# The expert-product stage of a two-block transformer kernel: gelu half a unit later, all low parts on VectorE, picks and token pairs spread over other blocks

## The chip, the cores and the metric

The kernel runs on one core of one Trainium2 chip. The metric is the device time of one execution in microseconds (us). Three runs of the kernel before gave 2947.26, 2949.1 and 2950.67 us.

## What is computed

The reference is a small model of two blocks for 256 tokens of width 2048. Nearly all of it is untouched here; the change lies in the last part, a feed-forward layer that takes for each token 16 of 16384 experts in each of 8 heads:

```python
q = (hf @ w_pq).reshape(T, PEER_HEADS, 2, PEER_HALF)
s1, s2 = ...                                     # scores against two sets of 128 keys
v1, i1 = lax.top_k(s1, 16); v2, i2 = lax.top_k(s2, 16)
cand = (v1[..., :, None] + v2[..., None, :]).reshape(T, PEER_HEADS, 256)
sc, ci = lax.top_k(cand, 16)                     # the picks
experts = e1 * 128 + e2                          # 128 experts per token
gates = softmax(sc)
...
u = jnp.take(w_u, experts); a = einsum('td,tkd->tk', h, u)
c = gates * gelu(a)
y = einsum('tk,tkd->td', c, jnp.take(w_v, experts))
```

## The kernel before

The kernel does not gather rows of `w_u`. It forms the product of all 16384 experts with all 256 tokens (this is the "u stage"), keeps gelu of it in a large table `C` of 128 partitions (first key of the expert) by 128 columns `e2` (second key) by 256 tokens, and multiplies the table by a sparse table of gates. After that, rows of `C` that are not empty are sent to memory in a compacted order, and their rows of `w_v` are gathered and multiplied.

**Units and blocks of the u stage.** The loop `u_block(e2)` runs over 128 units. A unit has two blocks `b` = 0 and 1, so there are 256 blocks; block `i` is `2 * e2 + b`. A block is a weight tile of 128 x 1024. It is loaded from `w_u` by SP into a buffer `wr`, ScalarE copies it to a rounded high part `wh` (L1464), and another engine subtracts to get the low part `wl` (L1469). There are four `wr`, two `wh` and two `wl` buffers. TensorE (PE) then runs eight matmuls of 512 columns with the high part and eight of 256 columns with the low part into a PSUM tile `P`. The high part of block `i + 1` is ordered by `split_next(i + 1)` at the start of block `i`, its low part by `low()` inside `between` of block `i`.

**End of a unit.** After its second block, ScalarE copies half of `P` to `a` (L1502, "the evacuation"), VectorE adds the other half (L1503), and GpSimd multiplies by the row scale (L1504; from the time when all gates are placed VectorE does it). `a` has two buffers, `rbc` and `junk`. The gelu of `a` is written by `tail()` (L1481 for tokens that have no gates yet, L1483 for the others, followed by a multiply into `C` at L1484 on GpSimd, later VectorE).

**`between`.** Once per block the kernel puts a portion of other work beside the matmuls:

- *Picks*: the top-16 searches on VectorE (L1350 to L1420), with the candidate sums on GpSimd (L1388). The generator gives a weight with each step: 45 for one head of 128 tokens (16 such) and 86 for the decoding of four heads (4 such), 1064 in all. A block takes steps until 18 units are used. Six further blocks hold the last of the gates' preparation (`finish`).
- *Pairs*: when the picks are done, each block makes one pair of tokens: `pair_ops` builds one-hot rows (six VectorE operations L1516 to L1518 and four ScalarE copies L1521 per pair), and the next block starts with `pair_mms`, eight small matmuls. Every second pair completes four tokens, and `quad_end` multiplies them into the rows of `C` that have their gelu (L1537 on VectorE) and copies the others (L1539 on ScalarE). 128 pairs take 128 blocks.
- *Places and sends*: when all 64 groups of four are done, `places` works out where the rows go, and GpSimd sends the rows of `C` (`send`, L1584), six per unit in the program, each waiting for nothing but its own row.

**The order of work** on PE, ScalarE and VectorE is the program order (`manual_schedule`): an instruction that waits holds up all behind it on its engine. GpSimd and SP have in-order queues of their own.

In the kernel before the low part of the second block of a unit is made by GpSimd while picks are under way, in seven units of eight; all others are made by VectorE.

Of the kernel before, what the change touches and what calls it, by code (L numbers as in the profile page):

```python
# [10 lines left out]
F32 = mybir.dt.float32  # L11
# [5 lines left out]
OP = mybir.AluOpType  # L17
# [1265 lines left out]
def peer(nc, tc, io, xd, hT, rbc, hp, sp, W, ident, mm, raw_block, split_block, proj_T, blocks, power_rstd, new_pair):  # L1283
    cd = io["cd"]
    with ExitStack() as es:
# [35 lines left out]
        with ExitStack() as pu_stack:  # L1321
# [132 lines left out]
            parts, tails, done = {}, [], [0]  # L1454
            q4 = 0

            def split_next(i):

                e2, b = divmod(i, 2)
                if e2 == 128:  # L1460
                    return lambda: None
                raw = raw_block(io["w_u"][e2, b])
                hi = W["pool"].tile([128, 1024], F32R, name="wh", bufs=W["hi"])
                nc.scalar.activation(hi, raw, AF.Copy)  # L1464
                eng = nc.gpsimd if b and not topk_done and e2 % 8 else nc.vector

                def low():
                    lo = W["pool"].tile([128, 1024], F32R, name="wl", bufs=W["lo"])
                    eng.tensor_tensor(lo, raw, hi.bitcast(F32), op=OP.subtract)  # L1469
                    parts[i] = hi, lo  # L1470

                return low

            def tail():

                if tails:
                    e2, a = tails.pop()
                    done[0] = e2 + 1
                    nt = 4 * q4
                    if nt < 256:  # L1480
                        nc.scalar.activation(C[:, e2, nt:256], a[:, nt:], AF.Gelu_apprx_tanh)  # L1481
                    if nt:
                        nc.scalar.activation(a[:, :nt], a[:, :nt], AF.Gelu_apprx_tanh)  # L1483
                        (nc.gpsimd if nt < 256 else nc.vector).tensor_tensor(  # L1484
                            C[:, e2, :nt], C[:, e2, :nt], a[:, :nt], op=OP.mult)

            def u_block(e2):
                P = pu.tile([128, 512], F32, name="pp")
                for b in range(2):
                    low = split_next(2 * e2 + b + 1)  # L1490
                    if b == 0:
                        tail()
                    between(low)
                    hi, lo = parts.pop(2 * e2 + b)
                    for j in range(8):
                        k = 8 * b + j
                        mm(P, hi[:, j * 128:(j + 1) * 128], hT[k].rearrange("p s t -> p (s t)"), k == 0, False)
                    for j in range(8):
                        k = 8 * b + j
                        mm(P[:, :256], lo[:, j * 128:(j + 1) * 128], hT[k][:, 0, :], False, k == KT - 1)  # L1500
                a = ua[e2 % 2]
                nc.scalar.activation(a, P[:, 256:], AF.Copy)  # L1502
                nc.vector.tensor_tensor(a, a, P[:, :256], op=OP.add)  # L1503
                (nc.gpsimd if q4 < 64 else nc.vector).tensor_tensor(a, a, rbc, op=OP.mult)  # L1504
                tails.append((e2, a))
# [3 lines left out]
            bank4 = [None]  # L1509
# [15 lines left out]
            def pair_mms(p, ws):  # L1525
                if p % 2 == 0:
                    bank4[0] = pq.tile([128, 4, 128], F32, name="pq")
                for i, w in enumerate(ws):
                    t = 2 * p + i
                    for a in range(3):  # L1530
                        mm(bank4[0][:, t % 4, :], w[:, 0, :], w[:, 1 + a, :], t % 4 == 0 and a == 0, t % 4 == 3 and a == 2)
                    mm(cnt[:, t // 128, :], w[:, 0, :], w[:, 4, :], t == 0, t == 255)

            def quad_end(q4, n):
                t4 = slice(4 * q4, 4 * q4 + 4)
                v = bank4[0].rearrange("p t e -> p e t")
                nc.vector.tensor_tensor(C[:, :n, t4], C[:, :n, t4], v[:, :n], op=OP.mult)  # L1537
                if n < 128:
                    nc.scalar.activation(C[:, n:, t4], v[:, n:], AF.Copy)  # L1539
# [50 lines left out]
            topk_done = False  # L1590
            left = 0
            pair, waiting = 0, []
            placing = None

            def between(low):


                nonlocal pair, q4, left, topk_done, placing
                if not topk_done or fins:
                    low()  # L1600
                    if fins and next(fins[0], "end") == "end":
                        fins.pop(0)
                        if topk_done:

                            nc.vector.tensor_scalar(C[:, :, 256:257].bitcast(I32).rearrange("p a o -> p (a o)"), iob,
                                                    128.0, row, op0=OP.mult, op1=OP.add)
                    left += 18
                    while left > 0 and not topk_done:
                        w = next(steps, None)
                        topk_done = w is None  # L1610
                        left -= w or 0
                    return
                full = None
                if waiting:
                    p, ws = waiting.pop()
                    pair_mms(p, ws)
                    if p % 2:
                        full = p // 2
                if pair < 128:
                    waiting.append((pair, pair_ops(pair)))  # L1620
                    pair += 1
                low()
                if placing and next(placing, "end") == "end":
                    placing = False
                if full is not None:
                    quad_end(full, done[0])
                    q4 += 1
                    if q4 == 64:
                        placing = places()
                        next(placing)  # L1630
# [68 lines left out]
        for i, e2 in enumerate(range(NC, 128)):  # L1699
            c2 = c_place()  # L1700
            halves(c2, C[:, e2, :256])
            for b in range(2):
                hi, lo = split_block(io["w_v"][e2 * 128:(e2 + 1) * 128, b * 1024:(b + 1) * 1024])
# [19 lines left out]
        def packed(j, tbs):  # L1723
            c2, v, off = fetch(j, tbs)
            for b in range(2):
                hi, lo = split_half(v, b)
                product(c2, b, hi, lo, tbs, off=off)
            return v

        def halves_of(j):  # L1730
            return tuple(tb for tb, (a, z) in enumerate((FIRST, SECOND)) if a <= j < z)
# [12 lines left out]
        for i, j in enumerate(order):  # L1744
            v = packed(j, halves_of(j))
# [7 lines left out]
        for i, j in enumerate(last_js):  # L1753
            c2, v, _ = fetch(j, (0, 1), vp.tile([128, 2, 256], F32R, name="lc", bufs=2))
# [9 lines left out]
        for tb in range(2):  # L1764
            t = slice(tb * 128, (tb + 1) * 128)
            y = xg[tb].rearrange("p (c n) -> p c n", c=4)
            ss = sp.tile([128, 2, 4], F32, name="xss", bufs=5)[:, 0, :]
            for c in range(4):
                for i, (c2, ws) in enumerate(last):
                    hi, lo = ws[c // 2]  # L1770
                    w = slice(c % 2 * 512, (c % 2 + 1) * 512)
# [119 lines left out]
```

## Time and profile before

| | us |
|---|---|
| median of three runs | 2949.1 |
| the profiled execution | 2950.48 |
| its span (first to last instruction) | 2948.7 |

| engine | busy in the span |
|---|---|
| PE (matmul) | 2768.1 us, 94% |
| VectorE (DVE) | 1898.4 us, 64% |
| ScalarE (ACT) | 1588.6 us, 54% |
| GpSimd (POOL) | 798.5 us, 27% |

The u stage lies between about 1537 and 2486 us of the span. A window of a stage gives for each engine the busy time in that stage; a wait is told as "who <- what it waited for"; in a timeline the number in brackets is the time that the engine sat idle just before, and what ended that. The clock PEclk is the share of the full clock that was granted to PE.

### The profile page before, as it was taken

The numbers are of one execution on the slowest core, as the hardware profiler recorded it, in microseconds if no ns is written. First come the engines' busy times: TensorE is split into PE (matmuls) and PEld (weight loads), VectorE is DVE, ScalarE is ACT, GpSimd is POOL, SyncE is SP. The second block draws the span as 40 slices with busy tenths as digits, with TensorE's granted clock in tenths as the row PEclk, the third lists the DMA queues.
The fourth block names the chain that finished last, engine by engine and source line by source line (L and its number), as shares of the span: only waits on it lengthen the run. The fifth ranks groups of instructions, "written<-read, shape, count | busy, mean of one in ns | idle before, by whom it ended". The sixth has DMA issues, their size and how long they took to land. (4 is left out here: it accounts for less than half of the span.)

```text
span 2948.7 us, 41341 instructions
## 1 busy us (share of the span) xinstructions
PE 2768.1 (94%) x14566; PEld 2301.3 (78%) x14566; DVE 1898.4 (64%) x3498; ACT 1588.6 (54%) x2951; POOL 798.5 (27%) x703
## 2 busy tenths in 40 slices
PE   8999999999999999999999899999994199999998
PEld 5867788887888888878887678888883087888886
DVE  7545576556766555565657878888882065766665
ACT  4445565445665544444544348888871054655554
POOL 6312320012310000111014442333337622322231
PEclk9999999999999999999999999999997599999999
DMA  6565443654446655666554344444445266988883
GB/s 224 177 223 189 134 139 123 218 187 154 147 144 208 209 183 167 215 211 193 183 179 157 134 157 158 159 158 161 160 144 189 98 216 236 359 298 285 299 308 133
DMA packets 158810, 561.74 MB, mean 191 GB/s; under 512 B 19584, under 2 KB 33536, under 8 KB 145024
## 3 DMA queue, kind: packets, MB, share of 16 engines
q1 hardware_dynamic: 137808, 433.71, 44.9%
q0 software_dynamic: 20784, 125.29, 11.4%
q8 instruction: 117, 1.92, 0.3%
q14 instruction: 101, 0.83, 0.1%
HBM read 531.17 MB, written 27.75 MB: 190 GB/s over the span
## 5 line engine op out<-in xcount | busy, mean ns | idle before, releaser
L204 DVE TENSOR_TENSOR wl<-wr,wh 128x1024 fp32r<-128x1024 f32 (+1 forms) x467 | 600.2, 1287 | 458.9 <-ACT wh L202 385.3
L187 PE MATMUL pp<-hT,wh 128*128 128x512 f32 x2880 | 754.4, 404 | 104.2 <-ACT wh L1464 53.3
L202 ACT ACTIVATE wh<-wr 128x1024 fp32r<-128x1024 f32 (+1 forms) x467 | 492.9, 1056 | 585.0 <-PE pp L187 495.5
L187 PE MATMUL pp<-wh,hT 128*128 128x512 f32 x2688 | 695.6, 399 | 4.6 <-ACT wh L202 2.7
L187 PEld LDWEIGHTS pp<-hT,wh 128*128 128x128 f32 x2880 | 525.0, 192 | 207.3 <-ACT wh L1464 58.8
L187 PEld LDWEIGHTS pp<-wh,hT 128*128 128x128 f32 x2688 | 501.3, 190 | 127.7 <-ACT wh L202 7.8
L187 PEld LDWEIGHTS pp<-hT,wl 128*128 128x128 f32 x2880 | 396.6, 192 | 57.8 <-issue 21.1
L187 PE MATMUL pp<-hT,wl 128*128 128x256 f32 x2880 | 406.6, 284 | 26.2 <-issue 20.3
L187 PE MATMUL pp<-wl,hT 128*128 128x512 f32 x1344 | 374.5, 400 | 12.1 <-DVE wl L204 12.1
L1469 DVE TENSOR_TENSOR wl<-wr,wh 128x1024 fp32r<-128x1024 f32 x230 | 278.7, 1221 | 116.3 <-issue 64.3
L187 PEld LDWEIGHTS pp<-wl,hT 128*128 128x128 f32 x1344 | 248.9, 190 | 70.6 <-DVE wl L204 15.4
L1464 ACT ACTIVATE wh<-wr 128x1024 fp32r<-128x1024 f32 x256 | 268.9, 1050 | 42.1 <-remote 33.1
L1676 ACT ACTIVATE hT<-vb 128x1024 fp32r<-128x1024 f32 x202 | 210.7, 1059 | 131.0 <-PE py L187 100.6
L1683 DVE TENSOR_TENSOR wr<-vb,hT 128x1024 fp32r<-128x1024 f32 x135 | 165.3, 1229 | 76.1 <-PE py L187 55.0
L1714 POOL DMA_INDIRECT vb<-w_v,cb x103 | 128.9, 1252 | 284.1 <-ACT hT L1676 99.7
L1584 POOL DMA_INDIRECT cd<-C,posi x124 | 137.6, 1110 | 138.0 <-DVE C L1484 89.5
L1521 ACT ACTIVATE oh<-oh,gP 128x128 bf16<-128x128 bf16 x512 | 162.0, 389 | 0.0
L187 PE MATMUL py<-hT,c 128*128 128x512 f32 x600 | 152.6, 389 | 0.0
L187 PE MATMUL py<-hT 128*128 128x512 f32 x592 | 150.4, 389 | 0.0
L187 PEld LDWEIGHTS py<-hT,c 128*128 128x128 f32 x600 | 112.6, 188 | 23.4
L187 PEld LDWEIGHTS py<-hT 128*128 128x128 f32 x592 | 111.1, 188 | 23.1
L1683 DVE TENSOR_TENSOR wl<-vb,hT 128x1024 fp32r<-128x1024 f32 x67 | 82.2, 1227 | 34.2 <-PE py L187 27.7
(445 smaller groups left out, 3162.4 us busy)
## 6 DMA issues: line engine op xcount, KB each, us to landing
wr<-w_u SPq DMA_DIRECT2D x256, 512.0 KB
wr<-w_even SPq DMA_DIRECT2D x104, 512.0 KB
wr<-w_out SPq DMA_DIRECT2D x96, 512.0 KB
wr<-w_odd SPq DMA_DIRECT2D x96, 512.0 KB
wr<-w_in SPq DMA_DIRECT2D x64, 512.0 KB
wr<-w_mem SPq DMA_DIRECT2D x32, 512.0 KB
wr<-w_pq SPq DMA_DIRECT2D x32, 512.0 KB
cb<-cd SPq DMA_DIRECT2D x103, 136.0 KB
```

What stands on the lines that cost most here:

```text
L187: nc.tensor.matmul(out, lhsT=lhsT, rhs=rhs, start=start, stop=stop, skip_group_check=True)
L202: nc.scalar.activation(hi, raw, AF.Copy)
L204: (lo_eng or nc.vector).tensor_tensor(lo, raw, hi.bitcast(F32), op=OP.subtract)
L1464: nc.scalar.activation(hi, raw, AF.Copy)
L1469: eng.tensor_tensor(lo, raw, hi.bitcast(F32), op=OP.subtract)
L1521: nc.scalar.activation(w[:, 1 + a, :], w[:, 4, :], AF.Copy, scale=gP[:, a, t:t + 1])
L1584: i = nc.gpsimd.indirect_dma_start(cd, bass.IndirectOffsetOnAxis(posi[:, e2:e2 + 1], 0), src, None).ins
L1676: nc.scalar.activation(hi, src, AF.Copy)
L1683: nc.vector.tensor_tensor(lo, src, hi.bitcast(F32), op=OP.subtract)
L1714: nc.gpsimd.indirect_dma_start(v, None, wide, bass.IndirectOffsetOnAxis(c[:, 256:257].bitcast(I32), 0))
```

## The change

The change has four parts, all in the u stage.

1. `tail()`, which writes the gelu of the unit before, is called in the second block of a unit instead of the first, again just behind the high part of the next block.
2. All low parts are made by VectorE.
3. The picks use 14 units per block instead of 18. By the weights they take 76 blocks (38 units) instead of 60, and the preparation of the gates ends at block 82 instead of 65.
4. Pairs start at block 83 instead of 66 and are spread so that 128 of them are made by block 193, the second block of unit 96. That is 111 blocks, of which 17 make two pairs. A block may start with two `pair_mms`. `pair_mms` returns its PSUM bank, since the next four tokens may already have begun another one when `quad_end` runs.

The last pair's matmuls stand at the start of block 194 in both kernels, and so do `places` and the first sends of the program.

```diff
@@ split_next
-                eng = nc.gpsimd if b and not topk_done and e2 % 8 else nc.vector
                 def low():
-                    eng.tensor_tensor(lo, raw, hi.bitcast(F32), op=OP.subtract)
+                    nc.vector.tensor_tensor(lo, raw, hi.bitcast(F32), op=OP.subtract)
@@ u_block
                     low = split_next(2 * e2 + b + 1)
-                    if b == 0:
+                    if b:
                         tail()
-                    between(low)
+                    between(2 * e2 + b, low)
@@ pair_mms, quad_end
+                return bank4[0]
-            def quad_end(q4, n):
+            def quad_end(q4, bank, n):
-                v = bank4[0].rearrange("p t e -> p e t")
+                v = bank.rearrange("p t e -> p e t")
@@ between
+            q_end = 2 * 97
-                    left += 18
+                    left += 14
...
-                full = None
-                if waiting:
-                    p, ws = waiting.pop()
-                    pair_mms(p, ws)
+                full, ws = [], list(waiting)
+                waiting.clear()
+                if pair < 128 and q_from is None:
+                    q_from = i
+                for p, w in ws:
+                    b4 = pair_mms(p, w)
                     if p % 2:
-                        full = p // 2
-                if pair < 128:
+                        full.append((p // 2, b4))
+                while pair < 128 and pair * (q_end - q_from) < 128 * (i + 1 - q_from):
                     waiting.append((pair, pair_ops(pair)))
                     pair += 1
                 low()
...
-                if full is not None:
-                    quad_end(full, done[0])
+                for p, b4 in full:
+                    quad_end(p, b4, done[0])
                     q4 += 1
```

## Rows read from the trace of the kernel before

**Rows 1.** Windows: picks, pairs, sends, rest; per engine busy us (instructions), clock, DMA.

```profile
1536.80:1769.00 232.20, 205.19 (x1112) 175.50 (x1111) 183.01 (x551) 96.62 (x147) 104.82 (x91) 0.96 0.45 150
1769.00:2195.00 426.00, 425.85 (x3075) 376.76 (x3073) 375.18 (x1026) 353.03 (x894) 144.18 (x126) 1.00 0.47 158
2195.00:2363.30 168.30, 63.79 (x311) 53.29 (x309) 36.49 (x59) 25.19 (x38) 105.81 (x106) 0.66 0.42 144
2363.30:2486.00 122.70, 122.70 (x705) 107.95 (x704) 78.98 (x113) 63.30 (x92) 33.54 (x20) 1.00 0.63 211
```

**Rows 2.** Timeline of PE: first high-part matmuls of blocks 0, 66 and 194.

```profile
1536.83 2.00 PE L187 MATMUL pp<-hT,wh 128*128 128x512 f32 x8
...
1769.03 1.32 PE L187 MATMUL pp<-hT,wh 128*128 128x512 f32 x5
...
2195.00 2.08 PE L187 MATMUL pp<-hT,wh 128*128 128x512 f32 x8
```

**Rows 3.** Waits while picks run (1536.8 to 1769 us): total us, times, longest.

```profile
ACT C L1481 <- POOL rbc L1504: 64.2, 16, 6.7
...
PE pp L187 <- ACT wh L1464: 26.5, 23, 3.4
...
DVE C L1350 <- POOL C L1388: 14.4, 10, 2.9
```

**Rows 4.** Timeline, all engines: from the end of unit 10 to block 24.

```profile
1613.88 0.40 DVE L1503 TENSOR_TENSOR rbc<-rbc,pp 128x256 f32<-128x256 f32 x1
...
1614.36 0.73 POOL L1504 TENSOR_TENSOR rbc<-rbc 128x256 f32<-128x256 f32 x1 [1.96 <-DVE rbc L1503]
...
1615.12 0.42 ACT L1481 ACTIVATE C<-rbc 128x256 f32<-128x256 f32 x1 [5.48 <-POOL rbc L1504]
...
1616.54 3.27 PE L187 MATMUL pp<-hT,wh 128*128 128x512 f32 x8 [2.20 <-ACT wh L1464]
```

**Rows 5.** Lines while picks run: busy us, mean ns of one, idle time before.

```profile
L1469 DVE TENSOR_TENSOR wl<-wr,wh 128x1024 fp32r<-128x1024 f32 x40 | 49.1, 1226 | 30.6 <-ACT wh L1464 30.6
L1417 DVE TENSOR_TENSOR C<-C 128x1024 bf16<-128x1024 bf16 x8 | 13.8, 1726 | 0.1
...
L1469 POOL TENSOR_TENSOR wl<-wr,wh 128x1024 fp32r<-128x1024 f32 x26 | 66.2, 2548 | 72.6 <-ACT wh L1464 72.6
```

**Rows 6.** Line L1417 by itself: shortest, median and longest ns.

```profile
L1417 DVE TENSOR_TENSOR C<-C x8: 684/1612/2895, 1576.9 to 1745.7; 128x1024 bf16<-128x1024 bf16 x8
```

**Rows 7.** Timeline, all engines, in one unit of the pair stage.

```profile
2175.30 0.42 DVE L1503 TENSOR_TENSOR junk<-junk,pp 128x256 f32<-128x256 f32 x1 [0.47 <-ACT junk L1502]
...
2175.80 0.79 DVE L1517 TENSOR_SCALAR oh<-iob,eT 128x128 bf16<-128x128 bf16 x1
...
2177.22 1.84 POOL L1484 TENSOR_TENSOR C<-C,junk 128x240 f32<-128x240 f32 x1 [0.68 <-ACT junk L1483]
...
2178.42 0.53 DVE L1537 TENSOR_TENSOR C<-C,pq 128x376 f32<-128x376 f32 x1
2178.87 0.24 DVE L1516 TENSOR_SCALAR oh<-iob,eT 128x128 bf16<-128x128 bf16 x1
2178.99 0.31 ACT L1539 ACTIVATE C<-pq 128x136 f32<-128x136 f32 x1 [0.73 <-DVE C L1537]
...
2180.12 1.26 ACT L1521 ACTIVATE oh<-oh,gP 128x128 bf16<-128x128 bf16 x4
2180.25 1.23 DVE L1469 TENSOR_TENSOR wl<-wr,wh 128x1024 fp32r<-128x1024 f32 x1 [0.19 <-ACT wh L1464]
...
2181.46 0.39 ACT L1502 ACTIVATE rbc<-pp 128x256 f32<-128x256 f32 x1
```

**Rows 8.** Timeline of the sends: the first, PE's longest idle time, the last back-to-back one.

```profile
2210.18 1.23 POOL L1584 DMA_INDIRECT cd<-C,posi  x1 [12.01 <-DVE more L1574]
...
2326.82 3.78 PE L187 MATMUL pp<-hT,wh 128*128 128x512 f32 x8 [42.77 <-issue]
...
2342.71 0.96 POOL L1584 DMA_INDIRECT cd<-C,posi  x1 [0.30 <-issue]
```

More of the change, by code (lines that the diff above doesn't have):

```diff
@@ L1592, in peer, with between @@
             pair, waiting = 0, []
-            placing = None
-            def between(low):
-                nonlocal pair, q4, left, topk_done, placing
+            placing = q_from = None
+            q_end = 2 * 97
+            def between(i, low):
+                nonlocal pair, q4, q_from, left, topk_done, placing
                 if not topk_done or fins:
```

## The prediction

> **What bounds the kernel now.** I read the windows of the u stage first, then the waits inside the window where PE is not busy, then a timeline at one such wait. In the windows [rows 1] PE is full while pairs are made (425.85 of 426.00 us) and in the rest at the end (122.70 of 122.70), so there only the amount of PE work counts. It is not full while picks are under way (205.19 of 232.20 us, granted clock 0.96 of the higher level) nor during the sends (63.79 of 168.30). The reader is to see that only these two stretches can give anything back.
>
> The price of a bare block comes from the last window: 705 matmuls are 44 blocks, in 122.7 us, so 2.79 us. The starts of blocks 0, 66 and 194 [rows 2] then say what is lost. Blocks 0 to 65 took 1769.03 - 1536.83 = 232.2 us where 66 x 2.79 = 184.1 would do: 48 us too much, the own small matmuls of the picks among it. Blocks 66 to 193 took 426.0 us for 128 blocks and 128 pairs; (426.0 - 128 x 2.79) / 128 = 0.54 us for the matmuls of one pair.
>
> In the picks window PE waits for one thing, the high part `wh`: 26.5 us in 23 waits [rows 3]. ScalarE, which makes it, sits in L1481, the gelu, waiting for GpSimd's product: 64.2 us in 16 waits for one of the two buffers of `a`. One such chain in the timeline [rows 4]: VectorE comes to the add L1503 at 1613.88, late because picks and a low part stand before it; GpSimd multiplies at 1614.36; the gelu starts at 1615.12 after 5.48 us of idle ScalarE; the high part stands right behind it, and PE starts block 24 at 1616.54 after 2.20 us idle. So the gelu holds up a high part that PE needs.
>
> **Part 1, the gelu half a unit later.** Removed: the high part of the next unit's first block no longer stands behind the wait. Now the evacuation and the high part after it do, and these are wanted one block, 2.79 us, later. The longest wait of the gelu was 6.7 us and PE's longest 3.4 [rows 3], so one block covers most of them. `tail` issues no DMA; it brings ScalarE's gelu and GpSimd's (later VectorE's) multiply with it, and SP's loads are moved past nothing. I cost it at nothing in the picks stage. In the pair stage it has a price, below.
>
> **Part 2, low parts on VectorE.** Removed: 26 low parts of 2.55 us on GpSimd. Added: VectorE makes every one, at 1.23 us each [rows 5]. VectorE was busy 183.0 us in the picks window [rows 1]. Take away its 40 low parts (49.1) and 33 adds of 0.41 (13.6, length as in [rows 7]): 120 us of picks and gate preparation. L1417 shows that some of this is waiting: its shortest run is 0.68 us and its longest 2.9 [rows 6], its mean 1.73 [rows 5], so 8 x 1.05 = 8 us go if the long ones lay beside GpSimd's low parts. That leaves 112.
>
> By the Trainium skill (SBUF — State Buffer, Who interferes with whom) GpSimd and a VectorE operation with two SBUF inputs take turns at a shared port pair, and the later one waits in full. The spread of L1417 agrees with that, and by it the 8 us would go whole. Against the change speaks the skill's Perfetto Trace Analysis, Optimizing Scalar/DVE Operations: a saturated VectorE may gain by giving work to GpSimd, though its next sentence doubts that between these two. By the first sentence alone, 33 low parts more on VectorE would be some 41 us lost; no run here shows it yet, and it is the case "picks do not speed up" below.
>
> **Part 3, picks over 76 blocks.** VectorE's sum there: 112 + 76 x 1.23 + 38 x 0.41 = 221 us, less about 5 of the second gate preparation, which falls into the six blocks after, and plus the waits for candidate sums. These were 14.4 us [rows 3] with GpSimd occupied by low parts; without, I take 8 (between 0 and 14). So 224 us on VectorE against 76 x 2.79 = 212 on PE. VectorE becomes the bound by a little, and the first 83 blocks cost 83 x 2.79 + 12 = 244 us. Bounds of the loss: 6 (every picks stall goes, PE keeps only its own extra matmuls) to 28 (no stall of VectorE goes).
>
> **Part 4, 17 more pairs squeezed in.** PE work is unchanged: 111 x 2.79 + 128 x 0.54 = 379 us from block 83 to 194. What is new is that ScalarE and VectorE must pass through a unit in time. I follow their order in one unit of before [rows 7]. The add L1503 starts at 2175.30, 0.47 us after the evacuation; pairs, low part and the four-token product (L1537 at 2178.42) run behind it without a gap; ScalarE's copy follows at 2178.99, then a high part, then four one-hot copies at 2180.12, 1.26 us, up to 2181.38, and the next evacuation at 2181.46. With the 0.47 this chain closes in 6.65 us, and a unit took 426.0 / 64 = 6.66 [rows 1]. There is no reserve in it.
>
> After the change the gelu stands in the last leg, between the high part and the one-hot copies. Its cost on ScalarE I take as 0.4 us, the length of one 256-element pass such as the evacuation [rows 7]. So where the four-token product falls into a unit's first block, a unit takes about 7.07. Where it falls into the second block the gelu is early, and only GpSimd's multiply L1484 (1.84 us in [rows 7]) may now meet the pair's operations on VectorE. L1517 shows what such a meeting costs: 0.79 where L1516 beside it takes 0.24 [rows 7], so 0.55. I take 0.15 on the mean, 6.8 a unit. Each double pair moves the four-token product to the other half, so half of the units are of each kind. The 17 units with a double pair carry a further pair on VectorE (2180.25 - 0.19 - 2178.87 = 1.19 us) and on ScalarE (1.26): about 8.0. Sum: 17 x 8.0 + 19 x 7.07 + 19.5 x 6.8 = 403 us, against 379: 24 us lost. I take 22, as the low parts made ahead absorb a little. Bounds: 0 (PE alone sets the pace) to 40 (0.55 in every unit of the second kind, and double pairs at 8.5).
>
> **The sends.** GpSimd sends rows back to back from 2210.18 to 2342.71, at 0.96 + 0.30 us each some 105 of them, and PE idles for up to 42.77 us in that time [rows 8]. The order of the sends starts at block 194 in both kernels, about as many rows are ready, and nothing in the diff slows the sends. I cost it at 0. What PE does in that stretch hangs on a few long waits; three blocks more or fewer are 8 us, which I keep for the range.
>
> **Sum.** First 83 blocks and pairs: 244 + 379 + 22 = 645 us, against 232 + 426 = 658. That is -13; with the fractions kept (-48 + 12 + 22) it is -14. The profiled execution took 2950.5, which gives 2936; it lies 1.4 above the median of the runs, so 2935.
>
> **Rivals.** *The pair stage holds PE's pace.* If VectorE and ScalarE run ahead far enough, the 22 become 5, and the time is 2949 - 48 + 12 + 5 = 2918. For it: the windows show VectorE busy 375 and ScalarE 353 of 426 us. Against it: the chain that closes in 6.65.
>
> *Picks stay bound by VectorE.* Its waits do not shrink, the loss is 28 instead of 12: 2949 - 48 + 28 + 22 = 2951, no change. For it: 224 against 212 leaves no reserve.
>
> *Slower: the pair stage slips.* GpSimd's multiply now starts beside the pairs' VectorE operations in every unit of the second kind, or the last leg of the chain grows in all. From 0.65 us more per unit over PE's 6.83 (379 / 55.5), that is 36 us, the gain is gone. With 1.84 us, the multiply's whole length, in half of the units, it is 24 + 28 x 1.7 = 72: 2949 - 48 + 12 + 72 = 2985. For it: L1517's 0.55. Against it: L1484 lies beside VectorE's work now too, and the stage is still PE's.
>
> *The change does not do what it says: picks do not speed up.* If VectorE's load, not the gelu's wait, is what delays the high part, a block of picks costs 232.2 / 66 = 3.52 as before: 76 x 3.52 + 7 x 2.79 + 379 + 22 = 688, +30: 2979. Against it: PE's waits there name `wh`, and the row of `wh`'s maker names GpSimd's product, not VectorE's load.
>
> **Chances and range.** My forecast (2935, with a band of 2922 to 2946) has 0.48; the pair stage at PE's pace 0.20; picks bound by VectorE 0.14; the pair stage slipping 0.11; no speed-up of picks 0.07. A measurement tells about 0.2%, 6 us, from no change. Faster by more than that: 0.42 of the first case, all of the second, 0.03 of the third: 0.65. Within: 0.05, and 0.11 of the third, and 0.02: 0.18. Slower: 0.17. The range for eight in ten reaches from the fast end of the second case with the sends' 8 us, 2910, to 2960, which takes in the third and leaves out most of the slow ones.
>
> **What the profile after would show.** The gelu's waits for GpSimd (64.2 us for one buffer) nearly gone, and PE's waits for `wh` in the picks stretch with them; blocks 0 to 83 in about 244 us with VectorE over 90% busy, and PE's remaining waits there naming `wl`; L1417 near 0.7 us. In the pair stretch a mean unit of 7.2 us, PE no longer full, with long units at double pairs and alternating stretches between. The sends as before: some 105 in a row and PE mostly idle for about 120 us. The forecast is wrong if the sends' stretch changes by more than 10 us, or if the pair stretch takes 6.8 or over 7.5 a unit.

## The result: 3.1% faster where the kernel before has an idle stretch, 0.5% slower where it has none

Beside the kernel before at 2949.3 us the kernel after took 2857.0 us (median of 4 runs, 2853.7 to 2864.6), a ratio of 0.969 [0.967, 0.971]. I had forecast 2935, between 2910 and 2960: the time fell outside the range. Then, in the experiments, the kernel before, unchanged, took 2844 to 2847 us in five groups of runs out of six, and beside 2845.5 the kernel after took 2860.5: 1.0052 [1.0038, 1.0066]. So most of the 92 us hang on something that the kernel before shows in some groups of runs and not in others, while the kernel after took nearly the same time in both. That the direction which I forecast came out in the first measurement was luck: where that something is absent, the change costs 15 us.

The spans divide as follows. Block starts and the last matmul of the u stage come from PE's records, as in [rows 2]; block 0 starts at 1536.8 us in both traces of the first measurement, and at 1538.4 and 1537.7 in `before_again` and `after_again`, the same kernels in a later group:

| stretch, us | before | after | change | before, again | after, again | change |
|---|---|---|---|---|---|---|
| blocks 0 to 193 | 658.2 | 637.7 | -20.5 | 660.1 | 637.4 | -22.7 |
| block 194 to the end of the u stage | 291.4 | 178.0 | -113.4 | 176.4 | 177.9 | +1.5 |
| from there to the end | 462.3 | 501.2 | +38.9 | 472.1 | 504.2 | +32.1 |
| sum | | | -95.0 | | | +10.9 |

The forecast of -14 was for the first line, which came out at -20.5 and -22.7. The second and third I had set to 0.

These windows of the kernel after (busy us of PE, PEld, DVE, ACT and POOL, clock, DMA share, GB/s) answer to [rows 1]: picks, pairs, sends, and the time behind the u stage.

```profile
1536.80:1769.00 232.20, 232.20 (x1351) 205.04 (x1350) 215.32 (x594) 123.64 (x178) 66.10 (x73) 1.00 0.56 184
1769.00:2174.00 405.00, 398.78 (x2830) 342.62 (x2829) 353.50 (x1009) 323.88 (x856) 81.44 (x111) 1.00 0.44 146
2200.00:2350.00 150.00, 150.00 (x862) 132.03 (x862) 98.90 (x139) 73.79 (x111) 125.02 (x83) 1.00 0.89 265
2352.00:2406.00 54.00, 11.37 (x52) 9.13 (x51) 5.64 (x8) 4.20 (x7) 37.26 (x38) 0.65 0.46 160
```

PE is full while picks run, 6 us short of full while pairs are made, full during the sends, where before it had 63.79 of 168.30 us, and then mostly idle behind the u stage. (A busy PE in this view need not be at its full rate: counted by blocks, the pair stage loses more, as told further down.) What it waits for there stands in the waits from 2352 to 2410 us (total us, times, longest):

```profile
PE py L187 <- ACT wh L202: 44.9, 1, 44.9
ACT c L1655 <- DMA wr<-w_u: 40.2, 1, 40.2
```

and, with a releaser that the profile names, in the timeline of all engines in `after_again`:

```profile
2394.17 0.96 POOL L1584 DMA_INDIRECT cd<-C,posi  x1 [0.30 <-issue]
2396.94 3.18 SPq L1715 DMA_DIRECT2D cb<-cd  x7
2399.15 0.42 ACT L1655 ACTIVATE c<-cb 128x256 fp32r<-128x256 f32 x1 [40.38 <-DMA cb<-cd]
```

`cb` is fetched from the memory that the sends fill, so SP issues the fetch only when the last send has landed (2396.61), and ScalarE starts on what was fetched. (In the first trace of the kernel after the wait is put down to "wr<-w_u", the last DMA on the same semaphore by the profile; its last send starts at 2393.56, and L1655 at 2398.40.) So the last send sets when the next stage starts. In the kernel after 92 of 124 sends leave in the u stage; the other 32 leave with PE mostly idle.

The picks stage is changed as forecast. Its waits (1536.8 to 1774.7 us, the end of block 82), against [rows 3]:

```profile
ACT C L1480 <- POOL rbc L1503: 10.1, 13, 1.3
...
DVE C L1350 <- POOL C L1388: 0.7, 3, 0.2
```

The gelu's wait for one buffer fell from 64.2 to 10.1 us, that for candidate sums from 14.4 to 0.7, and no wait of PE is left. L1417 by itself, against [rows 6]:

```profile
L1417 DVE TENSOR_TENSOR C<-C x8: 679/692/1231, 1582.1 to 1752.0; 128x1024 bf16<-128x1024 bf16 x8
```

### The profile page after: what moved, and what is told of

The parts are those of the page before. It is cut to its first block, busy times and chain, and to the rows that moved or that the text cites. A ratio compares the mean times of both kernels' runs of the same rounds, so it can differ in the third digit from the quotient of the medians.

```text
span 2853.7 us, 41401 instructions
## 1 busy us (share of the span) xinstructions
PE 2757.1 (97%) x14566; PEld 2289.3 (80%) x14566; DVE 1910.4 (67%) x3525; ACT 1583.8 (56%) x2943; POOL 725.9 (25%) x669
## 3 DMA queue, kind: packets, MB, share of 16 engines
q0 software_dynamic: 20784, 125.29, 11.7%
## 5 line engine op out<-in xcount | busy, mean ns | idle before, releaser
L187 PE MATMUL pp<-hT,wh 128*128 128x512 f32 x2880 | 736.8, 398 | 0.0
L187 PEld LDWEIGHTS pp<-hT,wh 128*128 128x128 f32 x2880 | 517.1, 189 | 94.4 <-issue 0.3
L1468 DVE TENSOR_TENSOR wl<-wr,wh 128x1024 fp32r<-128x1024 f32 x256 | 315.1, 1231 | 19.7 <-ACT wh L1464 17.7
L1584 POOL DMA_INDIRECT cd<-C,posi x124 | 168.1, 1356 | 50.4 <-issue 31.7
```

What stands on the lines that cost most here:

```text
L187: nc.tensor.matmul(out, lhsT=lhsT, rhs=rhs, start=start, stop=stop, skip_group_check=True)
L1468: nc.vector.tensor_tensor(lo, raw, hi.bitcast(F32), op=OP.subtract)
L1584: i = nc.gpsimd.indirect_dma_start(cd, bass.IndirectOffsetOnAxis(posi[:, e2:e2 + 1], 0), src, None).ins
```

## Experiments

All times stand beside the median of the kernel before in the same group of runs. "Last send" and block starts are from the traces.

**The gelu's place alone (tail_alone)**, put into the kernel before:

```
-                    if b == 0:
+                    if b:
                         tail()
```

> The kernel before with one edit: the gelu and its multiply are written in the second half of the next unit. Theory A (the move of the gelu parts the two low parts of a unit, so that two of four sends lie beside a low part on VectorE, sends fall from four to three a unit, and GpSimd's unbroken run of sends, during which PE idled from 2231 to 2357 us, never begins): sends of .96, 1.82 and 1.89 us in every unit; blocks 194 to 255 in about 178 us instead of 291; PE idle some 40 us more behind the u stage because the last sends land late; time 2949 - 113 + 39 = 2875, or 2860 to 2880 if the picks stage gains too. Theory B (another part of the change, or the place of the instructions in time, ended that idle stretch): it is still there, blocks 194 to 255 take 280 to 300 us, time 2935 to 2955.

2864.1 beside 2847.4: 1.0066 [1.0049, 1.0083]. Theory A's 2875 is near, but for the wrong reason: the kernel before took 2847 here and had no idle stretch to lose. What the edit does by itself shows clearly: blocks 0 to 65 in 207.8 us, 27 less than the 234.5 of `before_again`; the pair stage (blocks 66 to 193) 437.4 instead of 425.7; sends 1.81 us apart, last at 2400.7.

**The gelu's place undone (tail_undone, tail_undone_2)**, in the kernel after `if b:` becomes `if b == 0:`.

> The kernel after with the gelu and its multiply put back into the first half of the next unit; all else stays. Theory A: the low parts of a unit stand back to back again, four sends a unit, then the unbroken run with PE idle comes back: blocks 194 to 255 in about 290 us, the wait behind the u stage shrinks by 39; time 2857 + 113 - 39 = 2931, up to 2945 if the picks stage loses too. Theory B: no idle stretch, time 2850 to 2870.

2836.7 beside 2847.4: 0.9963 [0.9949, 0.9977]. Neither theory: no idle stretch, and 24 us less than the kernel after. The picks lose 15 us (blocks 0 to 82 in 253.0 instead of 237.9), but sends are 1.40 us apart, 116 of them leave in the u stage, the last at 2375.1. The same kernel in another group (tail_undone_2) took 2837.8 beside 2846.2; it was meant to tell Theory A from the rest where the kernel before takes 2950, and that it did not meet.

**One pair a block (one_pair)**, in the kernel after:

```
-                while pair < 128 and pair * (q_end - q_from) < 128 * (i + 1 - q_from):
+                if pair < 128:
```

> The kernel after with one pair of tokens a block again (pairs in blocks 83 to 210). Theory A: no idle stretch among the sends, three sends a unit. The pair stage loses nothing to PE's pace, as before (6.65 us a unit), so the u stage ends about 20 us earlier, at 2332; but the sends begin at about 2214 instead of 2189, 62 of 124 are out by 2332, the rest take 1.27 us each and end at 2410 instead of 2394, so that PE waits 80 us and the time is about 2872. Theory B, with the spread of the pairs as the cause: the idle stretch is back, time over 2920.

2860.8 beside 2847.4. The steps came as expected, u stage to 2336 (2332), last send 2413 (2410), PE mostly idle until then; the time came out 11 us under the 2872. The u stage ends 16 us before that of the kernel after, the last send leaves 19 us later, and the time is the same. So the end does not follow the u stage; it does not follow the last send to the microsecond either. Over the 16 traces without the stretch in which sends outlast the u stage, 449 to 463 us lie between the last send and the end, and 472 to 526 between the u stage and the end. Why three of them (one_pair among them) have 449 and the others 458 to 463 is open.

**A throttle that did not hold (three_sends, three_sends_2, seven_in_two)**, in the kernel before:

```
+        beat = pk.tile([128, 1], F32, name="beat")
...
-                    for _ in range(6):
+                    nc.gpsimd.tensor_copy(beat, C[:, e2 - 1, 0:1])
+                    for _ in range(3):
```

In seven_in_two the last line is `range(3 + e2 % 2)`.

> The kernel before with one edit: at most three sends a unit, behind a GpSimd copy of one element per partition that reads the row of C finished in that unit. Nothing else moves. Theory A (the pace of the sends causes the idle stretch): it is gone, blocks 194 to 255 in 175 to 185 us, sends end some 40 us after the u stage, time 2870 to 2880. Theory B (the pace of the sends is a consequence, the idle stretch has another cause): blocks 194 to 255 take 280 us or more, and with sends held back the end comes later still: 2950 to 2990.

> The kernel three_sends once more (before, at most three sends a unit behind a GpSimd copy that reads the unit's finished row). The kernel before took 2950 us beside some kernels and 2846 beside others, so chips differ in whether the idle stretch appears. Theory A2 (where it appears, it needs sends that leave GpSimd without a break; three a unit never start it): 2853 us here whatever the kernel before takes. Theory F (chips of the slow kind hold PE's releases up in this stretch in any kernel whose gelu stands in the first half, whatever the pace of the sends): beside 2950 of before, 2930 to 2960.

> As three_sends, with three and four sends in turn (3.5 a unit): GpSimd still gets a break in every second unit. If only a run without any break starts the idle stretch, none here: last send near 2213 + 124 / 3.5 x 5.58 = 2411 were no send faster, but after the u stage the rest goes at 1.27, so near 2388, time 2848 to 2853. If the stretch starts from a rate between three and four a unit, 2920 to 2960 where the kernel before takes 2950.

2853.1 beside 2847.4, 2856.1 and 2854.3 beside 2846.2. These say nothing of the pace: GpSimd's order is not written by hand, the copies went behind some 13 sends each, and 114 sends left in the u stage in all three, 1.43 us apart. The 6 to 10 us are the price of the copies and of a last send at 2392 to 2394.

**Both kernels again (before_again, after_again)**, unchanged.

> The kernel before, unchanged, on the chip of the experiments, where it took 2847 us beside the first four kernels and not 2949. Theory C (the 126 us in which PE idled among the sends belong to the executions that were measured first, not to the instructions of the kernel): picks and pair stages as in the first trace (blocks 0 to 193 in 658 us, within 3), but PE busy over 90% from 2195 to 2352 us, blocks 194 to 255 in 176 to 185 us, the last send near 2383, time 2842 to 2850. Theory A would want the idle stretch with every unthrottled run of sends.

> The kernel after, unchanged, on the chip of the experiments. Theory C: it does here what it did first, 2850 to 2862 us, so beside 2847 of the kernel before it gains nothing or loses up to 0.5%: 20 us won up to block 194, and more than that given back by three sends a unit, which put the last send near 2394. Theory A, that the change takes an idle stretch away, would want a gain of about 3% here too.

2848.9 and 2860.5 beside 2845.5. Theory C held, with the figures in the table above (the last send at 2385.7). The window of the sends in `before_again`:

```profile
2200.00:2350.00 150.00, 148.61 (x863) 130.71 (x862) 97.81 (x147) 74.84 (x108) 109.00 (x101) 1.00 0.84 277
```

PE is nearly full, by the same instructions that left it at 38% in [rows 1]. One stretch of GpSimd and VectorE then shows what the change does to the sends. GpSimd in `before_again`, one unit, against [rows 8]:

```profile
2231.15 0.96 POOL L1584 DMA_INDIRECT cd<-C,posi  x1 [0.30 <-issue]
2232.42 1.49 POOL L1584 DMA_INDIRECT cd<-C,posi  x1 [0.30 <-issue]
2234.21 0.96 POOL L1584 DMA_INDIRECT cd<-C,posi  x1 [0.31 <-issue]
2235.47 0.96 POOL L1584 DMA_INDIRECT cd<-C,posi  x1 [0.30 <-issue]
```

and VectorE beside it, the low parts in one row of two:

```profile
2231.51 0.43 DVE L1484 TENSOR_TENSOR C<-C,junk 128x256 f32<-128x256 f32 x1 [0.48 <-ACT junk L1483]
2231.85 2.35 DVE L1469 TENSOR_TENSOR wl<-wr,wh 128x1024 fp32r<-128x1024 f32 x2
```

The same in `after_again`, GpSimd:

```profile
2230.60 0.96 POOL L1584 DMA_INDIRECT cd<-C,posi  x1 [0.30 <-issue]
2231.86 1.81 POOL L1584 DMA_INDIRECT cd<-C,posi  x1 [0.30 <-issue]
2233.98 1.90 POOL L1584 DMA_INDIRECT cd<-C,posi  x1 [0.30 <-issue]
```

and VectorE:

```profile
2231.62 1.23 DVE L1468 TENSOR_TENSOR wl<-wr,wh 128x1024 fp32r<-128x1024 f32 x1
2233.48 0.43 DVE L1483 TENSOR_TENSOR C<-C,junk 128x256 f32<-128x256 f32 x1 [0.64 <-ACT junk L1482]
2233.83 1.22 DVE L1468 TENSOR_TENSOR wl<-wr,wh 128x1024 fp32r<-128x1024 f32 x1
```

A send that begins inside a low part ends 0.82 us after that low part (2231.86 + 1.81 against 2231.62 + 1.23; 2233.98 + 1.90 against 2233.83 + 1.22: 0.83). Over this trace 62 sends begin inside a low part, and they end 0.83 to 0.96 us after it, 0.83 at the median. Before, the two low parts of a unit are neighbours and catch one send. After, the gelu is later, so the product L1483 comes between them, and each catches one: three sends in 5.58 us instead of four.

**The gelu late, then early (late_then_early)**, in the kernel after:

```
+                late = q4 < 64
                 for b in range(2):
...
-                    if b:
+                    if b == late:
                         tail()
```

> The kernel after, but the gelu stands in the second half of the next unit only until the last pair is done, and from the next unit on in the first half, as before. If the gelu's place acts in the picks by the high part's wait and in the sends by parting the two low parts, both gains come together: blocks 0 to 82 in 238 us, blocks 0 to 193 in 638, sends at about 1.4 us each as in tail_undone, the last one near 2365 instead of 2394, 460 us more to the end: 2825, between 2815 and 2835. If the gelu's place does not set the pace of the sends, 2850 to 2860.

2828.3 beside 2845.5: 0.9939 [0.9926, 0.9953]. It confirms both halves: blocks 0 to 193 in 637.5, sends 1.40 us apart, the last at 2362.5, 462 us from there to the end.

**Low parts on GpSimd again (low_on_gpsimd)**, in the kernel after:

```
+                eng = nc.gpsimd if b and not topk_done and e2 % 8 else nc.vector
...
-                    nc.vector.tensor_tensor(lo, raw, hi.bitcast(F32), op=OP.subtract)
+                    eng.tensor_tensor(lo, raw, hi.bitcast(F32), op=OP.subtract)
```

> The kernel after with the low parts of the second blocks on GpSimd again during the picks (where the unit's number is no multiple of 8). By my prediction's step the VectorE operations beside them stall, some 8 us in all, and VectorE has 26 x 1.23 = 32 us less to do: blocks 0 to 82 in 235 to 248 us instead of 238, the rest unchanged, time within 10 us of the kernel after. If VectorE is the bound of the picks, as I took it, it is 6 us faster; if the shared port is, 8 us slower.

2875.0 beside 2845.5, 14.5 above the kernel after; blocks 0 to 82 in 257.0 us instead of 237.9. That is more than I gave the port. The lines while picks run (busy us, mean ns) show why:

```profile
L1469 DVE TENSOR_TENSOR wl<-wr,wh 128x1024 fp32r<-128x1024 f32 x43 | 87.3, 2029 | 11.8 <-ACT wh L1464 11.4
...
L1469 POOL TENSOR_TENSOR wl<-wr,wh 128x1024 fp32r<-128x1024 f32 x33 | 82.2, 2490 | 6.5 <-ACT wh L1464 6.5
```

In the kernel after the same VectorE pass takes 1.25 us:

```profile
L1468 DVE TENSOR_TENSOR wl<-wr,wh 128x1024 fp32r<-128x1024 f32 x83 | 104.0, 1253 | 7.9 <-ACT wh L1464 7.7
```

With low parts on GpSimd it takes 2.03 on the mean, that is 43 x 0.78 = 33 us more, which eats most of the 33 x 1.25 = 41 us that VectorE is spared. In that trace 25 of VectorE's low parts begin while GpSimd makes one, and each of them ends 1.08 or 1.09 us after GpSimd's, so it does nearly its whole work behind it. PE's waits in that kernel name GpSimd's low part (11.7 us in 16 waits).

**No low parts among the sends (no_low_in_sends)**, in the kernel before:

```
                 def low():
+                    if e2 >= 98:
+                        parts[i] = hi, hi
+                        return
```

> The kernel before, but from unit 98 on it makes no low parts: TensorE multiplies the high part where the low part stood, so the output loses that precision, and VectorE no longer runs a two-input pass of 1024 columns among the sends. Theory D (a run of sends that nothing slows holds up the releases that PE gives, and that is the idle stretch of the first trace): sends at .96 + .30 us without a break, PE's releases late by several us, blocks 194 to 255 in 250 us or more, time over 2900. Theory E (sends are slowed by VectorE's low part and that is all; the idle stretch needs something that this chip does not show): every send .96 us, the last one near 2212 + 124 x 1.27 = 2370 instead of 2386, PE busy over 95% from 2195 to 2352, the u stage ending at 2375 as before, time 2830 to 2845.

2949.0 in a single run, and here the kernel before beside it took 2950.2, as in the first measurement: the idle stretch is back. From 2216 to 2333 us every send takes 0.96 us, 1.26 apart, without a low part among them. PE's timeline, of 5.49 us of work and then 23 to 40 us of nothing:

```profile
2224.42 5.49 PE L187 MATMUL pp<-hT,wh 128*128 128x512 f32 x16 [3.87 <-issue]
2253.43 4.98 PE L187 MATMUL pp<-hT,wh 128*128 128x512 f32 x16 [23.51 <-issue]
2298.03 4.88 PE L187 MATMUL pp<-hT,wh 128*128 128x512 f32 x16 [39.62 <-issue]
```

The trace's semaphore events say what the word "issue" hides. The count that PE raises with its last matmul of a product lands 2.7, 22.1, 38.4 and 38.0 us after that matmul's end. In the first trace of the kernel before it is 0.7 us at 2228, then 0.8, 1.6, 6.7, 8.2, 17.8, 41.4 and 16.2, and it is over when the unbroken sends are. There PE's last matmuls before the longest idle time end at 2284.06, and the evacuation that waits for them starts at 2325.44 ("remote" is a release that the profile cannot place):

```profile
2281.98 2.08 PE L187 MATMUL pp<-hT,wl 128*128 128x256 f32 x8 [19.15 <-issue]
2325.44 0.38 ACT L1502 ACTIVATE junk<-pp 128x256 f32<-128x256 f32 x1 [66.08 <-remote]
```

In every trace without the stretch it is at most 0.02 us, wherever the trace has a record of it. The end of a matmul in the trace is modelled, so a late count and a last matmul that ended late look the same here. VectorE's low parts are no cause of the stretch. That favours Theory D, but the group differs from the others in more than this kernel.

**Eighteen steps of picks (eighteen_units)**, in the kernel after `left += 14` becomes `left += 18`.

> The kernel after with 18 steps of picks a block again instead of 14: the picks end some 17 blocks earlier, the pairs have 128 blocks and never come two to a block. By my prediction's sums VectorE needs 112 + 66 x 1.23 + 33 x 0.41 + 8 = 215 us for what PE does in 184, so 31 us are lost there instead of 12, and the 22 us that PE loses to double pairs go: blocks 0 to 193 in about 641 us against 635 to 638, the sends at three a unit as in the kernel after, time 2860 to 2870. If the loss in the pair stage comes from the late gelu and not from the double pairs, it stays: 655 us and 2875 to 2885.

2859.7 beside 2950.2: 0.9693 [0.9678, 0.9708]. In the very group in which the kernel before has the stretch, this one has none: sends of 0.96, 1.82 and 1.89 us, PE's count at most 0.02 us late. Blocks 0 to 193 took 642.5 (641 expected), 205.0 + 437.4: the loss in the picks was 21 and not 31 us, and 11 us were lost in the pair stage, against the kernel before, without a single double pair.

**The gelu late in the picks only (late_in_picks_only, late_in_picks_2)**, in the kernel after:

```
+                late = not topk_done or bool(fins)
...
-                    if b:
+                    if b == late:
...
-            q_end = 2 * 97
+            q_end = 2 * 93
```

> As late_then_early, but the gelu goes back to the first half as soon as the picks are done, and the pairs are spread to block 93 (in units) instead of 97. Picks as in the kernel after (238 us to block 83); pairs in 103 blocks: PE's own work 103 x 2.79 + 128 x 0.54 = 357, plus some 18 lost (tail_undone lost 16 in 111 blocks); so pairs end near 2150, sends begin near 2165 and at 1.4 us each the last is out at 2340, before the u stage ends at about 2348; 465 to 472 us from there to the end: 2813 to 2822. If the end did not follow from the last send, it would stay at 2828; if denser pairs cost more than 35 us, over 2830.

> The kernel late_in_picks_only once more, which took 2926 beside 2950 of the kernel before. Where before takes 2846, sends at 1.4 us from 2170 on are done at 2344, ahead of the end of the u stage near 2357, and the end no longer follows from them: 2357 + 465 to 470 = 2822 to 2827. Where before takes 2950, 2926 again with the idle stretch from about 2190.

2926.1 beside 2950.2, and 2820.2 beside 2844.1: 0.9913 [0.9897, 0.9930]. The same kernel, 106 us apart. Windows of the first and the second:

```profile
2250.00:2300.00 50.00, 2.07 (x8) 1.78 (x8) 1.23 (x1) 0.00 (x0) 38.11 (x40) 0.50 0.34 119
```

```profile
2200.00:2350.00 150.00, 150.00 (x860) 132.04 (x860) 95.53 (x138) 75.74 (x110) 111.54 (x102) 1.00 0.87 287
```

With the stretch, PE works 2 us of 50, and its count lands up to 41.4 us late. Without, the last send is out at 2341.2, before the u stage ends at 2353.4, and 465.7 us follow from that end and no longer from the sends. The group of the second shares its chip number with the group of the first, so the number alone doesn't tell the two kinds of group apart. (What does is told below.)

**Pairs to block 90 (pairs_to_90)**, in the kernel after `q_end = 2 * 90`.

> The kernel after with its pairs spread to block 90 (in units) instead of 97: 14 blocks fewer for 128 pairs, so 31 double units instead of 17. In one_pair, without doubles, blocks 83 to 210 lost 3 us to PE's work, in the kernel after 24, so a double costs 1.24: the u stage ends 17 us later, near 2369, pairs end 22 us earlier, and with three sends a unit the last send comes near 2372 instead of 2394. 460 us from there: 2832, between 2825 and 2845, on either kind of chip, since three sends a unit start no idle stretch.

2839.9 beside 2846.2: 0.9976 [0.9967, 0.9985], 20 us under the kernel after. The 14 further doubles cost 15.4 us (blocks 83 to 193 in 415.2 us against 399.8), 1.1 each where 1.24 was expected, and the last send came at 2379 instead of 2372.

**A throttle that holds (three_sends_held)**, in the kernel before; and **late_in_picks_held**, the same edit in late_in_picks_only:

```
-                    for _ in range(6):
+                    nx = posi[:, sent[0]:min(sent[0] + 3, NC)]
+                    nc.vector.tensor_copy(nx, nx)
+                    for _ in range(3):
...
             tail()
+            nx = posi[:, sent[0]:]
+            nc.vector.tensor_copy(nx, nx)
```

> The throttle of three_sends did not hold: GpSimd's order is not written by hand there, most of its copies went behind the sends, and 114 sends left in the u stage as in the kernel before. Here each group of three sends waits for a VectorE copy of its three columns of row numbers, which is written behind the unit, so three a unit is the most. All else is the kernel before. 29 units make 87 sends by 2375, the other 37 at 1.27 us end at 2422, 460 us from there: 2882. Theory A2 (the pace of the sends alone starts the idle stretch on chips that show it): 2882 also where the kernel before takes 2950, and PE busy over 95% from 2200 to 2350. Theory F (there it comes with the gelu in the first half, whatever the pace): 2930 or more beside 2950. Where before takes 2846, 2882 too: a last send 36 us later costs 36 us.

> late_in_picks_only with its sends held to three a unit, each group behind a VectorE copy of its three columns of row numbers, as in three_sends_held. From 2170 on 100 sends are out by 2357, the rest by 2387, 460 us from there: 2840 to 2847. Theory A2: this also where the kernel before takes 2950 and late_in_picks_only took 2926, with PE busy over 95% from 2200 to 2350. Theory F: there it stays within 20 us of 2926, or above. Where before takes 2846, the 20 to 27 us above late_in_picks_2 are the price of the slower pace.

2874.4 beside 2844.1: 1.0106 [1.0089, 1.0124]; and 2837.8 beside 2845.7: 0.9973 [0.9962, 0.9983]. Sends and last send came as expected (87 in the u stage and 2422.9; 99 and 2388.7), the times 8 and 2 us under the expectation. Both ran where the kernel before took 2846, so they price the slower pace: 30 us above the kernel before for a last send 37 us later, and 18 us above late_in_picks_2, whose end did not hang on the sends. They say nothing on the idle stretch.

## Why the prediction was wrong, and where it was right

**The step that failed** is the one on the sends: "The order of the sends starts at block 194 in both kernels, about as many rows are ready, and nothing in the diff slows the sends. I cost it at 0." Something in the diff slows them. I had followed the moved gelu through the picks and the pair stage, with GpSimd's multiply, but not into the sends, where that multiply is VectorE's and stands between the two low parts. There it turns four sends a unit into three. What I put at 0 measured -113.4 us from block 194 to the end of the u stage and +38.9 behind it, -74.5 in all, where the kernel before has the stretch, and +1.5 and +32.1 where it has not. In the second case this is the whole result: 22.7 us won by block 194, and a last send at 2394 instead of 2386, 32 us more behind the u stage.

The second fault of the same step is its price for uncertainty, 8 us for "three blocks more or fewer". PE was idle for 104 of 168.3 us in [rows 1], and the trace gave "issue" as the reason, that is none. An idle time of this size without a cause can go as well as stay, and the range should have reached to 2949 - 14 - 104, with some of it given back. None of my four rivals touched it.

**What starts the idle stretch is not settled.** In the two groups that had it, the kernels divide by one thing: the kernel before, no_low_in_sends and late_in_picks_only (sends 1.26 to 1.33 us apart in the stretch) have it, and eighteen_units (1.82) has not; nor had the kernel after (1.82) in its first measurement beside 2949. In the other groups no kernel had it, at 1.40 us apart too. So, as far as these five kernels tell, it needs the fast sends (or the early gelu, which went with them in each of these kernels) and a condition from outside the kernel. In the kernel before and in late_in_picks_only the sends begin at 1.4 to 1.5 us apart, as in the other groups, and reach 1.26 only as PE falls idle and low parts stay away, so there the fast pace is in part an effect. The throttled kernels, which part pace and gelu, never met that condition. GpSimd without a break is not enough: in the kernel after it has none either.

The condition left a mark in the traces. In the five traces of those two groups, with the stretch and without, records of DMA landings are missing: 17192 to 17858 of them stand there, where each of the other fifteen traces has 18944. The loss lies among the sends: up to 2100 us the kernel after has 12160 in its first trace and in `after_again`, from 2200 to 2400 us 1929 against 2874. The list of DMAs from 2200 to 2350 us shows it for the kernel after, in its first measurement and in `after_again`: with records missing it gives no time from issue to landing.

```profile
cd<-C,posi POOLq DMA_INDIRECT x83
```

```profile
cd<-C,posi POOLq DMA_INDIRECT x84, 5.4
```

So the kernel after and eighteen_units met the condition and stayed without the stretch. It also leaves a rival that no run tests: that the recording of events falls behind on such an occasion and itself holds up PE's counts. Then the stretch would belong to the measurement and not to the work. No run on record parts the two.

**Picks** (forecast 244 us to block 83, 12 lost): 237.9, of which 83 x 2.79 = 231.6 are PE's, so 6.3 lost, the lower bound that I gave. VectorE was busy 215.3 of 232.2 us, 93%, as I wrote, but "VectorE becomes the bound by a little" was wrong: no PE wait names `wl`. The size of part 2 was wrong too. I gave it the 8 us of L1417, which went (0.69 us at the median now); taking GpSimd's low parts away, with the gelu late, is worth 19 us, because VectorE's own low parts would then take 2.03 us. In the trace of before they took 1.23 [rows 5]. With the late gelu alone (tail_alone, blocks 0 to 65) VectorE's begins inside one of GpSimd's 11 times instead of once, and takes 1.50:

```profile
L1469 DVE TENSOR_TENSOR wl<-wr,wh 128x1024 fp32r<-128x1024 f32 x40 | 59.9, 1501 | 4.8 <-ACT wh L1464 4.6
```

So the early gelu kept the two apart, and the second edit is worth more with the first than it would be alone. By the Trainium skill (SBUF — State Buffer, Who interferes with whom) a VectorE instruction with two SBUF inputs and a GpSimd one that reads SBUF share a port pair, and the later blocks in full; 2.03 against 1.25 agrees, the passes that end 1.08 us behind GpSimd's above all, and so does the send that waits for the end of a low part.

**Part 1** at nothing in the picks was about right: alone it brings 27 us there (tail_alone), and with the other parts in place 15 (tail_undone). **Part 4**: 21 us lost from block 83 to 193 (399.8 against 378.8), 22 forecast. The terms: units of the first kind 6.83 and not 7.07 (tail_alone and eighteen_units, 437.4 / 64), of the second 6.72 and not 6.8 (one_pair, 430.4 / 64 from block 83), so the double pairs cost about as I had them, 1.1 to 1.2 us each (pairs_to_90: 36 us for 31).

**Rivals.** The pair stage neither kept PE's pace (2918) nor slipped (2985), the picks were not bound by VectorE (2951), and they did speed up (2979). Their stage was right and is 20.5 us in all; the deciding stage was another.

**A version that beats both** where the kernel before takes 2846 is late_in_picks_2 at 2820. Where it takes 2950, the kernel after's 2857 and eighteen_units' 2860 beat its 2926. pairs_to_90, with three sends a unit and 2840, is under both kernels in the first case; in the second it wasn't tried.

## What to carry to other kernels

Follow a moved operation into every stage in which its loop runs, and there ask what it now stands between: the gelu was looked at where it waited, and it cost where it did not. Find the last event that the next stage needs (here the last send, with 449 to 463 us behind it) and price each edit by what it does to that. And where the profile shows a long idle time without a releaser, measure the kernel before again before costing anything there, since the stretch may not belong to the kernel; and see whether records are missing from its trace.

## What the runs showed of the hardware

A row send from GpSimd takes 0.96 us and 0.30 to the next. One that begins while VectorE makes a low part, a pass with two SBUF inputs, ends 0.83 us after that pass (median of 62 in `after_again`, at most 0.96); the pass itself isn't lengthened (1.22 us). The Trainium skill (SBUF — State Buffer, Who interferes with whom) says of this kind of pass that it was not seen to stall a DMA, and marks the reason as inferred; here it does, 1.81 and 1.90 us against 0.96. These sends take their row numbers from SBUF, and the section's rule on GpSimd instructions that read SBUF, drawn on above, would cover them.

A VectorE low part that begins while GpSimd makes one ends 1.08 or 1.09 us after GpSimd's (25 of 25 in low_on_gpsimd); alone it takes 1.22.

PE's semaphore counts, which land within 0.02 us of the matmul's end as the trace models it, came up to 41 us late in three traces, while sends went out 1.26 to 1.33 us apart. Two of the three kernels ran on another occasion too and showed none of it, and it moved their time by about 104 and 106 us. What differs between the occasions isn't known, except that records of landings are missing from every trace of the one kind.
